# Low parts of the activations on GpSimd in four pieces, the second group's halves in the v part, 22 v passes beside u, and the samples' rstd a quarter step later

## The chip, the cores and the metric

One core of a Trainium2 chip. The metric is the device time of one execution in microseconds; it was 3186.38 for the kernel before (median of three). TensorE is PE, its weight loads PEld, VectorE DVE, ScalarE ACT, GpSimd POOL, SyncE SP.

## The reference

One decoder layer for 512 prompt tokens and 8 x 8 sample tokens (D = 2048), then a final RMSNorm. Cut to what matters here:

```
h  = rmsnorm(x) * (1 + scale1) + shift1;  x = x + gate1 * mix(h)      # RG-LRU and short conv, 1 projection in, 1 out
h2 = rmsnorm(x) * (1 + scale2) + shift2
# PEER: 8 heads, product keys 128 x 128 -> 16384 experts, top 16 per head
q    = (h2 @ w_q) per head, two halves of 128;  scores against 128 + 128 sub keys;  top 16 of the 256 sums
g    = softmax(top);  act = gelu(<h2, expert_u[eidx]>) * g
x    = x + gate2 * sum_k act_k * expert_v[eidx_k]
y    = rmsnorm(x)
```

expert_u and expert_v are 16384 x 2048 in fp32. All matrix products must come out in fp32 accuracy.

## The kernel before

The first 1160 us or so compute modulation, projections, scans and the output projection. The two parts after that hold the change.

**u part** (to about 2220 us). Of the 128 blocks of 128 experts, the L = 80 that the prompt's tokens pick most are computed densely. A block's rows of `ut` come in two half blocks n (0 to 159, NU2 = 160). `load` brings a half block into `raw` (SP queue, L892, 512 KB). `conv` splits it for PE, whose fp32r products are made of three passes: ACT writes the high part `xhi` (L908), POOL the low part `xlo = raw - xhi` (L909). `ahead(l, c)` issues loads up to l and conversions up to c, in order. `u_half` (L1405) multiplies 8 tiles three times each (hi*hi, hi*lo, lo*hi), 24 matmuls of 512 columns a half block. ACT applies gelu and writes the block's activations to DRAM (`actd`).

**Sparse rest.** Tokens whose picks lie in the other blocks, and the samples, are done by passes: POOL gathers 128 rows of 8 KB (`take`, L1235, an indirect DMA), DVE makes the dot product with h in a u pass (L1263), or adds the weighted row to `accB`, which is in PSUM, in a v pass (L1290). There are 219 uses of the u kind (NU; 214 of them are passes), then 214 v passes. `gather_to(k)` issues uses up to pass k, with gathers as far ahead as row buffers are free. From half block R2 = 129 on the passes are spread evenly: from G0 = 201 to NU + EARLY_V at the u part's end.

**v part** (from about 2220 us to 3151). M = 80 steps m of four quarter steps kq. A step takes four blocks and a quarter of the 2048 columns, as two half blocks n = 160 + 2m and the next; a quarter step is 12 matmuls (`v_column`, L1425), where the stationary side is `xhi` or `xlo` and the moving side the blocks' activations, `ahi` and `alo`. `v_sum` adds a finished bank to `acc` (DVE, L1447). Activations come in groups sg of four blocks (SG = 4, 20 groups). A group's work is a row of jobs, keyed by quarter step 4m + kq:

- `load_weights(sg, q)`, four loads of the gates into `gsb` (ACT queue, L1356); `load_acts(sg, q)`, two loads of the activations into `actr` (ACT queue, L1363). Both tiles have one buffer.
- `weigh(sg)`: `actr *= gsb` on DVE (L1368), three quarter steps before `halve`.
- `halve(sg, 0)`: `ahi` on ACT (L1375); `halve(sg, 1)`: `alo = actr - ahi` on DVE (L1379). `ahi` and `alo` have three buffers.

With h_ the quarter step of `halve(sg, 0)` (12, 28, 44, ... 284 for sg 2 to 19), `hi_at` is that of the group before. Groups 0 and 1 are done at the end of the u part, at half blocks 153, 154 and 158, 159. A step issues first its `ahead`, then at each quarter step the passes due there, the jobs, and the matmuls. Each engine's queue keeps the order of the code. The passes of the v part are spread by `room`, which takes WEIGH = 2.8 off a quarter step that is in `busy`.

**The tail.** `fplan` names the quarter steps at which the samples' end (`finish_b`) goes on by one piece. Its fifth piece is the matmul that spreads the samples' rstd (`token_norm`: `ph` from `rcfb`, L1474); `rcfb` is computed on DVE and ACT (L144 to L150) from the sums of the fourth (L1469). `last` is 73. In the last steps `load_x` brings the residual `xf` (into the buffers of `gsb` and `actr`) and `add_x` adds it on DVE (L1440).

Of the kernel before, what the change touches and what calls it, by code (L numbers as in the profile page):

```python
# [32 lines left out]
SG = 4  # L33
# [17 lines left out]
LAG = 4  # L51
FIRST_G = 6
PAIRS = 8
EARLY_V = 16
KEPT = 5
WEIGH = 2.8
PARTS = 2
# [20 lines left out]
def r32(ap):  # L78
    return ap.bitcast(F32)


def build(ctx, tc, A, O, dbg=None):
    nc = tc.nc
    V, S, PE, G = nc.vector, nc.scalar, nc.tensor, nc.gpsimd
# [792 lines left out]
    raws, parts, gsb, ahl, acts, pools = {}, {}, {}, {}, {}, {}  # L877
# [36 lines left out]
    def ahead(l, c):  # L914
        while at["l"] <= min(l, len(stream) - 1):
            load(at["l"])
            at["l"] += 1
        while at["c"] <= min(c, len(stream) - 1):
            conv(at["c"])
            at["c"] += 1  # L920
# [114 lines left out]
    def sample_twice():  # L1035

        for k0 in range(0, KD, 8):
            r, a = new_row(f"dup{k0}")
            row_log[a] = True
            d = r.bitcast(F32R).rearrange("p (q k t) -> p q k t", q=2, t=128)  # L1040
            dups.append(d)
            for q in range(2):
                S.activation(d[:, q].rearrange("p k (r t) -> p k r t", t=NG),
                             r32(hv[q][:, k0:k0 + 8, None, NA:T]).to_broadcast([128, 8, 2, NG]), AF.Copy)
# [306 lines left out]
    def load_weights(sg, q):  # L1351

        if q == 0:
            gsb[sg] = ep.tile([128, NCH, SG * TC], F32, name=f"gsb{sg}", tag="gsb", bufs=1)
        c = slice(q * NCH // GP, (q + 1) * NCH // GP)
        nc.scalar.dma_start(gsb[sg][:, c, :], gd[c, :, sg * SG:(sg + 1) * SG, :].rearrange("c p i t -> p c (i t)"))  # L1356
# [13 lines left out]
    def halve(sg, part):  # L1370

        if part == 0:
            pool = ep if sg % 3 < 2 else pools["vx"]
            hi, lo = (pool.tile([128, SG, NA], F32R, name=f"{x}{sg}", tag=f"{x}{sg % 3}", bufs=1) for x in ("ahi", "alo"))
            S.activation(hi, acts[sg], AF.Copy)  # L1375
            ahg[sg] = (hi, lo)
            return
        hi, lo = ahg[sg]
        V.tensor_sub(lo, acts.pop(sg), r32(hi))  # L1379
        for j in range(SG):  # L1380
            ahl[SG * sg + j] = (hi[:, j, :], lo[:, j, :])

    ahg = {}
# [259 lines left out]
    for n in range(NU2):  # L1643
        _, i, c = stream[n]
        if n == 0:
            sample_twice()
        if n == 1:
            sample_rows()
        ahead(n + 3, n + 2)
        spare += PIECE if R1 is None else PIECE_G  # L1650
        if R1 is not None:
            put(2)
            g_one(n)
            if not gk:
                g_start()
            elif gm[0] < min(upto(n), gm[1] + PAIRS - 1):
                g_pair(gm[0])
                gm[0] += 2
                spare -= 2.2
            while gm[2] < gm[3]:  # L1660
                g_scale(gm[2])
                gm[2] += 1
            gm[3], gm[4] = gm[4], gm[0]

        even, waits = R2 is not None, False
        while spare > 0 and R2 is None:
            cost = next(steps1 if R1 is None else steps2, "end")
            if cost == "end":
                if R1 is None:
                    R1 = n  # L1670
                else:
                    R2 = n
                break
            if cost is None:
                waits = True
                break
            spare -= cost
        if not even:
            if since is None and ready[0]:
                since = n  # L1680
            if since is not None and n == since + 1:
                fetch_to(RB - 1)
            if since is not None and n > since + 2:
                due_g += RATE[R1 is not None] + (0.7 if waits and spare > 4.5 else 0.0)
            g0 = gu[0]
            gather_to(due_g, ready[0])
            if gu[0] == ready[0] and sorted_[0]:
                fetch_to(gu[0] + 1, ready[0])
            due_g = min(due_g, gu[0] + 1.0)
            spare -= 2.4 * (gu[0] - g0)  # L1690
            if waits:
                spare = min(spare, 3.0)
            G0 = gu[0]
        else:
            gather_to(G0 + (NU + EARLY_V - G0) * (n - R2) // (NU2 - 1 - R2))
        if n == E0:
            assert not pair and not stg
            put(len(puts))
            p2.close()
            epx = ctx.enter_context(ExitStack())  # L1700
            ep = epx.enter_context(tc.tile_pool(name="ep", bufs=1))
        u_half(n, i, c)
        for sg, o in ((0, 1), (1, 7)):
            d = n - E0 - o
            if 0 <= d < 2:
                load_weights(sg, 2 * d)
                load_weights(sg, 2 * d + 1)
            if 2 <= d < 4:
                load_acts(sg, d - 2)
            if d == 5 - sg:  # L1710
                weigh(sg)
            if d == 6 - sg:
                halve(sg, 0)
            if d == 7 - sg:
                halve(sg, 1)
    hp_.close()
    vp = ctx.enter_context(tc.tile_pool(name="vp", bufs=1, side="right"))
    acc = vp.tile([128, KD, NA], F32, name="acc")
    pools["vx"] = ctx.enter_context(tc.tile_pool(name="vx", bufs=1, side="right"))
    NV0 = NU + EARLY_V  # L1720
    gather_to(NV0)
# [3 lines left out]
    last = M - VQ - ENDS  # L1725
    KQ = KD // VQ
    jobs, busy = {}, {}
    hi_at = -4
    for sg in range(2, L // SG):
        use = uses_of[sg * SG]  # L1730
        free = KQ * (uses_of[(sg - 3) * SG][-1] + 1) if sg >= 3 else 0
        h_ = min(KQ * use[0] - 7, max(free, hi_at + 16))
        assert h_ >= free and h_ >= hi_at + 13, (sg, h_, free, hi_at)
        for q in range(GP):
            jobs.setdefault(max(hi_at - 1 + q, 0), []).append(lambda sg=sg, q=q: load_weights(sg, q))
        for q in range(AP_):
            jobs.setdefault(max(hi_at + 5 + q, 0), []).append(lambda sg=sg, q=q: load_acts(sg, q))
        jobs.setdefault(h_ - 3, []).append(lambda sg=sg: weigh(sg))
        jobs.setdefault(h_, []).append(lambda sg=sg: halve(sg, 0))
        jobs.setdefault(h_ + 2, []).append(lambda sg=sg: halve(sg, 1))  # L1740
        busy[h_ - 3] = busy[h_ + 2] = WEIGH
        hi_at = h_
    room = {}
    for m in range(last):
# [1 line left out]
            room[m, kq] = PIECE / 2 - 0.75 * steps[m][4] - busy.get(KQ * m + kq, 0.0)  # L1746
    tot, run_ = sum(room.values()), 0.0
    fb = finish_b()
    fplan = {(last, 3), (last + 1, 2), (last + 1, 3), (last + 2, 1), (last + 2, 2), (last + 2, 3)}
    fin["tok"] = []  # L1750
    tplan = {(last + 1, 1), (last + 1, 2), (last + 1, 3), (last + 2, 0)}
    NT = len(uses)
# [2 lines left out]
    for m in range(M):  # L1755
        gi, q, bl, first, final = steps[m]
# [56 lines left out]
    with tc.If(any_ > 0), tc.tile_pool(name="fb", bufs=1) as fp:  # L1813
        io1 = fp.tile([128, 128], F32, name="f_io1")
        V.tensor_scalar(io1, iota, 1.0, None, op0=ALU.add)
        for i, (p0, n, c) in enumerate(GT):
# [18 lines left out]
            d = fp.tile([128, NPK], F32, name=f"f_d{i}", tag="d", bufs=1)  # L1835
            a = fp.tile([128, D], F32, name=f"f_a{i}", tag="a", bufs=1)
# [105 lines left out]
```

## Time and profile before

| | |
|---|---|
| runs | 3186.25, 3186.38, 3189.34 us |
| profiled execution | 3178.14 us |
| its span | 3176.2 us |
| mean granted clock of PE | 0.985 |
| u passes' dots, v passes' adds, DVE | 483.2 us (x214), 475.2 us (x202) |
| xlo, POOL, whole program | 773.8 us (x320) |
| alo and weigh, DVE | 20 each, medians 2.29 and 2.29 us |
| ahi, ACT | 20, median 1.90 us |

The profile is that of one execution, whose time lies 8.2 us below the median of the runs; its rows add up to its own time. An engine's row gives busy time, share of the span, and instructions. A group's row gives count, busy time, the mean in ns, and the idle time of the engine ahead of it with what ended it. A row of waits gives what an engine stood for: total us, times, longest. A window's row gives start and end, length, busy time of PE, PEld, DVE, ACT and POOL with their counts, the granted PE clock, the DMA share, and GB/s.

### The profile page before, as it was taken

Reading aid. Unit: us, or ns where it says so; the run is one execution under the profiler, and the core shown is the slowest. Engines: PE = TensorE matmul, PEld = TensorE weight load, DVE = VectorE, ACT = ScalarE, POOL = GpSimd, SP = SyncE. Lnnn points to the kernel's source line nnn. Section 1 sums busy time; section 2 is a strip of 40 time slices with the busy share of each in tenths; the row PEclk is TensorE's granted clock in tenths of the full one; section 3 lists DMA queues with packets and bytes.
Section 4 is the critical chain, followed back from the end, with each engine's and each line's share of the span. In section 5 each row is a group of like instructions: output and inputs, shape, how many; then the busy total and the mean of one; then the engine's idle time right before and its main releaser. Section 6 shows DMA issues by size and latency. Waiting matters only on the chain.

```text
span 3176.2 us, 46544 instructions
## 1 busy us (share of the span) xinstructions
PE 3060.1 (96%) x17239; PEld 2604.4 (82%) x17239; DVE 2123.5 (67%) x3240; ACT 1047.0 (33%) x1640; POOL 1681.4 (53%) x983
## 2 busy tenths in 40 slices
PE   5999999999989999999999999999999999999997
PEld 2688888899979998887888888887788888787776
DVE  3455621143254797986998999945677888888765
ACT  3234311123232223222555555652322222222222
POOL 2333333344333335667565666645766767777752
PEclk9999999999999999999999999999999999999998
DMA  9743566633332126989889999979999999899984
GB/s 386 281 138 136 180 206 212 214 127 131 126 114 102 67 82 216 310 307 384 339 333 387 393 380 393 384 278 373 380 382 356 380 376 376 302 388 378 374 294 154
DMA packets 294473, 882.81 MB, mean 278 GB/s; under 512 B 34998, under 2 KB 76854, under 8 KB 242774
## 3 DMA queue, kind: packets, MB, share of 16 engines
q1 hardware_dynamic: 160608, 380.39, 33.5%
q0 software_dynamic: 63744, 413.40, 32.7%
q10 hardware_dynamic: 69888, 86.00, 7.6%
q8 instruction: 136, 2.23, 0.3%
q14 instruction: 97, 0.79, 0.1%
HBM read 861.02 MB, written 66.81 MB: 292 GB/s over the span
## 4 chain that ended last, share of the span: by engine, by line
PE 68%; DMA 14%; POOL 6%; issue 5%; DVE 5%; ACT 1%; SPq 1%; ACTq 0%; POOLq 0%; DVEq 0%
PE pu L1405 17%; PE pv L1425 17%; PE pp_o L140 6%; DMA raw<-v 4%; DMA gsb<-gd 4%; PE pp_c L140 3%; PE pp_s L140 3%; POOL xlo L909 3%; PE qa L140 3%; PE pp_b L140 3%; PE qb L140 3%; PE pp_x L140 2%; PE pp_y L140 2%; PE ada L190 2%; DMA actr<-actd 2%
## 5 line engine op out<-in xcount | busy, mean ns | idle before, releaser
L909 POOL TENSOR_TENSOR xlo<-raw,xhi 128x1024 fp32r<-128x1024 f32 x320 | 773.8, 2427 | 424.2 <-ACT xhi L908 414.5
L908 ACT ACTIVATE xhi<-raw 128x1024 fp32r<-128x1024 f32 x320 | 338.1, 1061 | 862.5 <-PE pv L1425 311.4
L1263 DVE SCALAR_TENSOR_TENSOR u<-u,hT 128x2048 f32<-128x2048 f32 x214 | 483.2, 2282 | 104.3 <-DMA u<-u,rows 103.9
L1290 DVE SCALAR_TENSOR_TENSOR accB<-v,dots,accB 128x2048 f32<-128x2048 f32 x202 | 475.2, 2353 | 102.2 <-DMA v<-v,rows 99.0
L1425 PE MATMUL pv<-ahi,xhi 128*128 128x512 f32 x1280 | 509.6, 398 | 8.2 <-DVE acc L1447 5.4
L1405 PE MATMUL pu<-hhi,xhi 128*128 128x512 f32 x1280 | 515.0, 402 | 0.0
L1425 PE MATMUL pv<-ahi,xlo 128*128 128x512 f32 x1280 | 507.3, 396 | 6.3 <-POOL xlo L909 6.2
L1405 PE MATMUL pu<-hhi,xlo 128*128 128x512 f32 x1280 | 503.3, 393 | 1.6 <-POOL xlo L909 1.5
L1425 PE MATMUL pv<-alo,xhi 128*128 128x512 f32 x1280 | 504.2, 394 | 0.0
L1405 PE MATMUL pu<-hlo,xhi 128*128 128x512 f32 x1280 | 503.6, 393 | 0.0
L1235 POOL DMA_INDIRECT u<-u,rows x214 | 214.7, 1003 | 206.5 <-DVE u L1263 154.2
L1425 PEld LDWEIGHTS pv<-ahi,xlo 128*128 128x128 f32 x1280 | 242.2, 189 | 64.9 <-POOL xlo L909 8.7
L1425 PEld LDWEIGHTS pv<-ahi,xhi 128*128 128x128 f32 x1280 | 242.2, 189 | 64.5 <-DVE acc L1447 7.7
L1405 PEld LDWEIGHTS pu<-hhi,xlo 128*128 128x128 f32 x1280 | 241.1, 188 | 57.0 <-POOL xlo L909 2.8
L1425 PEld LDWEIGHTS pv<-alo,xhi 128*128 128x128 f32 x1280 | 242.6, 190 | 54.7
L1405 PEld LDWEIGHTS pu<-hhi,xhi 128*128 128x128 f32 x1280 | 241.7, 189 | 49.6 <-issue 0.9
L1405 PEld LDWEIGHTS pu<-hlo,xhi 128*128 128x128 f32 x1280 | 241.9, 189 | 48.5
L1235 POOL DMA_INDIRECT v<-v,rows x214 | 246.3, 1151 | 51.8 <-issue 33.9
L1599 ACT ACTIVATE op<-op,it 128x128 f32<-128x128 f32 x512 | 155.6, 389 | 40.3 <-DVE op L1591 40.2
L1605 PEld LDWEIGHTS gbank<-wr,op 128*128 128x128 f32 x1024 | 133.1, 191 | 21.4 <-ACT stg L1612 11.9
L1447 DVE TENSOR_TENSOR acc<-acc,pv 128x512 f32<-128x512 f32 x144 | 96.9, 682 | 76.7 <-PE pv L1425 76.7
L129 POOL TENSOR_TENSOR wlo_o<-raw_o,whi_o 128x1024 fp32r<-128x1024 f32 x32 | 77.5, 2423 | 119.9 <-ACT whi_o L127 115.9
(498 smaller groups left out, 5453.5 us busy)
## 6 DMA issues: line engine op xcount, KB each, us to landing
wa<-w_ada SPq DMA_DIRECT2D x96, 1024.0 KB, 7.5
raw<-ut SPq DMA_DIRECT2D x160, 512.0 KB, 7.9
raw<-v SPq DMA_DIRECT2D x320, 256.0 KB, 9.0
actd<-act ACTq DMA_DIRECT2D x80, 256.0 KB, 7.5
gd<-stg ACTq DMA_DIRECT2D x64, 320.0 KB, 12.3
gsb<-gd ACTq DMA_DIRECT2D x80, 256.0 KB, 14.4
actr<-actd ACTq DMA_DIRECT2D x40, 512.0 KB, 9.7
raw_o<-w_out SPq DMA_DIRECT2D x32, 512.0 KB, 3.4
```

Of the source, the lines that this page charges most:

```text
L129: lo_engine(share).tensor_sub(lo, raw, r32(hi))
L140: PE.matmul(o, st, mv[pick](k), start=first, stop=last)
L908: S.activation(hi, raw, AF.Copy)
L909: G.tensor_sub(lo, raw, r32(hi))
L1235: G.indirect_dma_start(out=out, out_offset=None, in_=src, in_offset=bass.IndirectOffsetOnAxis(ap=idx, axis=0), bounds_check=NE * 128 - 1, ...
L1263: V.scalar_tensor_tensor(r, r, 1.0, st["h"], op0=ALU.mult, op1=ALU.mult, accum_out=dots[i][:, j:j + 1])
L1290: V.scalar_tensor_tensor(st["a"], r, dots[i][:, j:j + 1], st["a"], op0=ALU.mult, op1=ALU.add)
L1405: PE.matmul(pu, st[:, kk, :], movA[mv](k), start=k == 0 and a == 0, stop=k == KD - 1 and a == 2)
L1425: PE.matmul(pv, st, mv, start=first and j == 0 and a == 0, stop=last and not end and j == SG - 1 and a == 2)
L1447: V.tensor_add(ak, ak, pv)
L1599: S.activation(ops[:, j0 + j, :], ops[:, j0 + j, :], AF.Copy, scale=it[2][:, b * 4 + j:b * 4 + j + 1])
L1605: PE.matmul(pg[:, j * L:(j + 1) * L], ops[:, j0 + j, :], wr[:, j0 + j, :], start=True, stop=True)
```

## The change

1. `EARLY_V` is 22 instead of 16: six more v passes end beside the u part (from n = 129 on 40 passes instead of 34), and 192 gathers of v remain after it instead of 198.
2. `halve`'s low part is made by POOL in pieces of one block (128 x 512), two pieces as part 1 and two as part 2 (L1380).
3. In the u part only group 0 is halved, at half blocks 153, 154 and 155. Group 1 is halved at quarter steps 1, 2 and 3 of the v part.
4. `hi_at` starts at -1 instead of -4, so `halve` comes a quarter step later for every group from 2 on (13, 29, 45, ... 285), at h_, h_ + 1 and h_ + 2. The gates' loads stand at hi_at - 1 + q, which are now the four quarter steps of one step (before, the first fell into the step ahead). `busy` holds weigh alone.
5. `fplan` has the samples' rstd at (last + 2, 3) instead of (last + 2, 2), and the piece after it at (last + 3, 1).

```diff
-EARLY_V = 16
+EARLY_V = 22
...
@@ halve
         hi, lo = ahg[sg]
-        V.tensor_sub(lo, acts.pop(sg), r32(hi))
-        for j in range(SG):
+        for j in range(SG // 2 * (part - 1), SG // 2 * part):
+            G.tensor_sub(lo[:, j, :], acts[sg][:, j, :], r32(hi[:, j, :]))
             ahl[SG * sg + j] = (hi[:, j, :], lo[:, j, :])
@@ u part, for sg, o in ((0, 1), (1, 7)): d = n - E0 - o
-            if d == 6 - sg:
-                halve(sg, 0)
-            if d == 7 - sg:
-                halve(sg, 1)
+            if 6 <= d < 9 and not sg:
+                halve(sg, d - 6)
@@ jobs of the v part
-    hi_at = -4
+    hi_at = -1
+    for a in range(3):
+        jobs.setdefault(1 + a, []).append(lambda a=a: halve(1, a))
...
-            jobs.setdefault(max(hi_at - 1 + q, 0), []).append(lambda sg=sg, q=q: load_weights(sg, q))
+            jobs.setdefault(max(hi_at - 1 + q, q), []).append(lambda sg=sg, q=q: load_weights(sg, q))
...
-        jobs.setdefault(h_, []).append(lambda sg=sg: halve(sg, 0))
-        jobs.setdefault(h_ + 2, []).append(lambda sg=sg: halve(sg, 1))
-        busy[h_ - 3] = busy[h_ + 2] = WEIGH
+        for a in range(3):
+            jobs.setdefault(h_ + a, []).append(lambda sg=sg, a=a: halve(sg, a))
+        busy[h_ - 3] = WEIGH
...
-    fplan = {(last, 3), (last + 1, 2), (last + 1, 3), (last + 2, 1), (last + 2, 2), (last + 2, 3)}
+    fplan = {(last, 3), (last + 1, 2), (last + 1, 3), (last + 2, 1), (last + 2, 3), (last + 3, 1)}
```

In the rows below the number behind a name is that of the half block, the group or the pass (`xlo157` is that of half block 157, `alo0` that of group 0, `v0_13` a gathered row of v); the number behind the underscore tells buffers apart. `x2` is two such instructions in a row.

POOL at the end of the u part, before:

```order
L909 TENSOR_TENSOR xlo157_20197<-raw157_20149,xhi157_20196 128x1024
L1235 DMA v0_13_20200<-v,rows0_8654 128x2048
L909 TENSOR_TENSOR xlo158_20240<-raw158_20191,xhi158_20239 128x1024
L1235 DMA v0_14_20243<-v,rows0_8654 128x2048
L909 TENSOR_TENSOR xlo159_20284<-raw159_20234,xhi159_20283 128x1024
```

and now:

```order
L909 TENSOR_TENSOR xlo156_20180<-raw156_20122,xhi156_20179 128x1024
L1235 DMA v0_17_20183<-v,rows0_8654 128x2048
L1380 TENSOR_TENSOR alo0_20169<-actr0_19994,ahi0_20168 128x512 x2
L909 TENSOR_TENSOR xlo157_20223<-raw157_20174,xhi157_20222 128x1024
L1235 DMA v0_18_20226<-v,rows0_8654 128x2048
L1380 TENSOR_TENSOR alo0_20169<-actr0_19994,ahi0_20168 128x512 x2
L909 TENSOR_TENSOR xlo158_20268<-raw158_20217,xhi158_20267 128x1024
L1235 DMA v0_19_20271<-v,rows0_8654 128x2048
L1235 DMA v0_20_20276<-v,rows0_8654 128x2048
L909 TENSOR_TENSOR xlo159_20317<-raw159_20262,xhi159_20316 128x1024
```

Two pieces of group 0 have come between `xlo156` and `xlo157`, two between `xlo157` and `xlo158`, and the gathers are those of four to six passes later.

DVE in the v part about group 13 (about 2745 to 2770 us), before:

```order
L1368 TENSOR_TENSOR actr13_24683<-actr13_24683,gsb13_24524 128x2048
L1290 SCALAR_TENSOR_TENSOR accB1_23993<-v1_27_24717,dots1_14473,accB1_23993 128x2048
L1290 SCALAR_TENSOR_TENSOR accB1_23993<-v1_28_24774,dots1_14473,accB1_23993 128x2048
L1290 SCALAR_TENSOR_TENSOR accB1_23993<-v1_29_24792,dots1_14473,accB1_23993 128x2048
L1447 TENSOR_TENSOR acc_20421<-acc_20421,pv6_4_24854 128x512
L1290 SCALAR_TENSOR_TENSOR accB1_23993<-v1_30_24849,dots1_14473,accB1_23993 128x2048
L1447 TENSOR_TENSOR acc_20421<-acc_20421,pv6_5_24868 128x512
L1379 TENSOR_TENSOR alo13_24951<-actr13_24683,ahi13_24950 128x2048
L1447 TENSOR_TENSOR acc_20421<-acc_20421,pv6_6_24886 128x512
L1447 TENSOR_TENSOR acc_20421<-acc_20421,pv6_7_24906 128x512
```

and the group's pieces now, on POOL:

```order
L909 TENSOR_TENSOR xlo256_24972<-raw256_24705,xhi256_24971 128x1024
L909 TENSOR_TENSOR xlo257_24976<-raw257_24792,xhi257_24975 128x1024
L1235 DMA v3_3_25012<-v,rows3_8660 128x2048
L1380 TENSOR_TENSOR alo13_25018<-actr13_24750,ahi13_25017 128x512 x2
L1235 DMA v3_4_25050<-v,rows3_8660 128x2048
L1305 DMA accd_8628<-v1_32_24859,tok_8651 512x2048
L1380 TENSOR_TENSOR alo13_25018<-actr13_24750,ahi13_25017 128x512 x2
L909 TENSOR_TENSOR xlo258_25076<-raw258_24801,xhi258_25075 128x1024
L909 TENSOR_TENSOR xlo259_25080<-raw259_24885,xhi259_25079 128x1024
```

`alo13` has left DVE, where it stood between two sums of finished banks, for POOL, where it follows the step's two xlo and precedes those of the next.

PE in step 75 (`pv9_13` and `pv9_14` are its quarter steps 1 and 2), before:

```order
L1425 MATMUL pv9_13_27531<-ahi18_26879,xhi311_27494 128x512
L1425 MATMUL pv9_13_27531<-alo18_26880,xhi311_27494 128x512
L1425 MATMUL pv9_13_27531<-ahi18_26879,xlo311_27495 128x512
L1474 MATMUL ph_27544<-ident_76,rcfb_27642 128x64
L1425 MATMUL pv9_14_27567<-ahi18_26879,xhi310_27490 128x512
```

and now:

```order
L1425 MATMUL pv9_14_27627<-ahi18_26951,xhi311_27554 128x512
L1425 MATMUL pv9_14_27627<-alo18_26952,xhi311_27554 128x512
L1425 MATMUL pv9_14_27627<-ahi18_26951,xlo311_27555 128x512
L1474 MATMUL ph_27604<-ident_76,rcfb_27702 128x64
L1425 MATMUL pv9_15_27646<-ahi18_26951,xhi310_27550 128x512
```

The matmul that spreads the rstd stands behind the 12 of quarter step 2 instead of the 12 of quarter step 1.

## The prediction

> **What bounds the kernel now.** I read the engine totals first, then windows of the last stage, then what TensorE waited for, then the chain at those places. The engine totals of the page:
>
> ```profile
> PE 3060.1 (96%) x17239; PEld 2604.4 (82%) x17239; DVE 2123.5 (67%) x3240; ACT 1047.0 (33%) x1640; POOL 1681.4 (53%) x983
> ```
>
> PE is busy for 96% of the span, so an edit off PE can win only what PE waits, and what its clock loses behind a wait. All edits lie between 2050 us and the end. The windows there (window, length, busy us of PE, PEld, DVE, ACT, POOL with counts, granted clock, DMA share, GB/s):
>
> ```profile
> 2120.00:2140.00 20.00, 20.00 (x101) 16.84 (x100) 5.72 (x6) 6.62 (x9) 11.22 (x8) 1.00 0.62 205
> 2200.00:2220.00 20.00, 19.91 (x87) 15.98 (x86) 10.31 (x5) 6.89 (x7) 13.85 (x8) 1.00 1.00 373
> 2220.00:2240.00 20.00, 16.81 (x60) 12.85 (x59) 11.92 (x6) 5.23 (x7) 13.94 (x8) 0.83 0.93 349
> 2300.00:2340.00 40.00, 40.00 (x175) 32.58 (x174) 29.53 (x20) 10.30 (x9) 26.76 (x18) 1.00 1.02 386
> 2620.00:2660.00 40.00, 40.00 (x175) 32.57 (x175) 36.65 (x20) 9.68 (x10) 34.64 (x21) 1.00 0.95 361
> 2740.00:2780.00 40.00, 35.47 (x141) 28.04 (x140) 31.73 (x16) 9.46 (x9) 27.86 (x17) 0.91 0.91 330
> 2860.00:2900.00 40.00, 37.99 (x162) 30.01 (x162) 31.87 (x18) 8.02 (x7) 26.54 (x18) 1.00 0.99 373
> 3020.00:3060.00 40.00, 36.24 (x155) 28.60 (x154) 34.11 (x20) 10.30 (x9) 26.91 (x14) 1.00 0.81 309
> 3080.00:3100.00 20.00, 17.04 (x73) 13.66 (x73) 9.71 (x17) 3.19 (x5) 6.84 (x3) 0.91 0.66 214
> ```
>
> An undisturbed window holds 175 matmuls in 40 us, 0.2286 us each; a step of 48 is 11.0 us, a group's four steps (192) are 43.9 us. Missing matmuls are lost time: 34 in 2740:2780 (7.8 us), 20 in 3020:3060 (4.6), 13 in 2860:2900 (3.0), 27.5 in 2220:2240 (6.3). What PE waited for between 2160 and 3160 us (us in total, times, longest):
>
> ```profile
> PE pv L1425 <- POOL xlo L909: 6.2, 4, 1.7
> PE pv L1425 <- DVE acc L1447: 5.4, 3, 3.5
> PE ph L1474 <- DVE rcfb L150: 3.0, 1, 3.0
> PE pv L1425 <- ACT xhi L908: 2.6, 3, 1.5
> ```
>
> That is all there is to win: 17.2 us of waits, and the clock behind the longest: 0.83 of 20 us (3.4 us lost), 0.91 of 40 (3.6), 0.91 of 20 (1.8). So 26 us at most, less at most whatever the change adds.
>
> **The change, part by part.** The sum stands against the profiled execution, 3178.1 us, which is 8.2 under the median 3186.4; I add the 8.2 back at the end.
>
> *The samples' rstd behind 12 more matmuls.* The chain at that place (start, us):
>
> ```profile
> 3070.12 14.02 DMA xf<-x1d
> 3084.16 0.75 DVE acc L1440
> ...
> 3086.19 0.43 PE ph L1474 x2
> 3086.62 10.09 PE pv L1425 x36
> ...
> 3097.60 2.79 PE pv L1425 x12
> ```
>
> PE stood 3.0 us at L1474 since rcfb on DVE followed acc L1440, which followed a transfer. Then 36 matmuls took 10.09 instead of 3 x 2.79 = 8.4: 1.7 us of clock. With 12 more matmuls ahead the wait shrinks by 2.79 to 0.2; 2860:2900, with waits of 1.7 and less, kept a clock of 1.00. Nothing else in the tail waits for ph within a quarter step. -4.5 (ends: 0 if the transfer lands 3 us later, -4.7).
>
> *alo off VectorE.* Around the longest wait, DVE's rows, then POOL's, then one link of the chain:
>
> ```profile
> 2757.99 2.36 DVE L1290 SCALAR_TENSOR_TENSOR accB<-v,dots,accB 128x2048 f32<-128x2048 f32 x1 [3.11 <-DMA v<-v,rows]
> 2760.25 0.68 DVE L1447 TENSOR_TENSOR acc<-acc,pv 128x512 f32<-128x512 f32 x1
> 2760.85 6.53 DVE L1379 TENSOR_TENSOR alo<-actr,ahi 128x2048 fp32r<-128x2048 f32 x1
> 2767.30 1.27 DVE L1447 TENSOR_TENSOR acc<-acc,pv 128x512 f32<-128x512 f32 x2
> ```
>
> ```profile
> 2760.49 4.74 POOL L909 TENSOR_TENSOR xlo<-raw,xhi 128x1024 fp32r<-128x1024 f32 x2
> 2765.38 2.87 POOL L1235 DMA_INDIRECT v<-v,rows  x1 [0.16 <-issue]
> ```
>
> ```profile
> 2719.80 25.07 DMA actr<-actd
> ```
>
> alo stood ahead of two acc that PE needed for its banks, and took 6.53 us because POOL's two xlo ran until 2765.2; the gather behind them took 2.87 while alo ran. With alo elsewhere the acc comes at 2760.9 instead of 2767.3, and the 3.5 us wait goes with its clock (3.5 of the 3.6). The other two waits on acc, 1.9 us, I leave: no row puts them behind alo. What is late next is weigh, for which actr's 25 us landing is as late as before; it holds VectorE, but acc is then one accB behind, not one alo. -7 (ends: -2, when that landing alone decides; -9.0, all of 5.4 and 3.6).
>
> *alo on GpSimd.* Prices (groups, and the tile):
>
> ```profile
> L909 POOL TENSOR_TENSOR xlo<-raw,xhi 128x1024 fp32r<-128x1024 f32 x320 | 773.8, 2427 | 424.2 <-ACT xhi L908 414.5
> L1235 POOL DMA_INDIRECT v<-v,rows x214 | 246.3, 1151 | 51.8 <-issue 33.9
> L318 POOL TENSOR_TENSOR w1hs<-w1r,w1xc 128x512 fp32r<-128x512 f32 x4 | 5.1, 1277 | 29.7 <-ACT w1xc L317 29.7
> ```
>
> ```profile
> L1379 DVE TENSOR_TENSOR alo<-actr,ahi x20: 2283/2290/6528, 2194.6 to 3037.2; 128x2048 fp32r<-128x2048 f32 x20
> ```
>
> L318 is the same subtraction in a piece's size: 4 x 1.28 = 5.1 us a group, for 2.29 on VectorE. GpSimd's densest window is 2620:2660, 34.64 of 40, so 38.0 of a group's 43.9; with the pieces 43.1. It gets back what alo took from it, 1.9 where a gather took 2.87 for 0.99: 41.2 of 43.9. Elsewhere (26.76 of 40) there is more room. While it waits for ahi, its xlo would wait too, but the next xhi stands behind that ahi on ScalarE anyway. So nearly hidden. The last pieces are issued five quarter steps (13.7 us) ahead of their first matmul or more, and three (8.2 us) ahead of the next load into actr, which has one buffer. With the gsb loads issued in one step in place of two: +1.5 (ends: 0, and +25 below).
>
> *Six passes fewer in the v part.* 214 passes less 16 are 198 there; less 22, 192. Six are 6 x 128 rows x 8 KB = 6.3 MB, 16 us of the transfers at 386 GB/s, in some 850 us of a stage in which they run at 0.9 to 1.0: 2% less. PE's waits on xlo and xhi are 8.8 us, of which 3.2 lie at the transition (below); the other 5.6 come from raw that landed late, and can shrink. -3, about half, since 2% shortens a queue that is just full by more than 2% (ends 0, -5.6). The passes move into the last 170 us of the u part, where 2120:2140 has a DMA share of 0.62 and DVE 5.72 of 20: nothing, up to the last 20 us, which are at 1.00.
>
> *The transition.* ScalarE's rows, GpSimd's, and one link of the chain:
>
> ```profile
> 2203.08 0.34 ACTq L1363 DMA_DIRECT2D actr<-actd  x1
> 2203.46 1.06 ACT L908 ACTIVATE xhi<-raw 128x1024 fp32r<-128x1024 f32 x1 [2.16 <-POOL xlo L909]
> ...
> 2221.46 1.06 ACT L908 ACTIVATE xhi<-raw 128x1024 fp32r<-128x1024 f32 x1 [3.89 <-DMA raw<-v]
> ```
>
> ```profile
> 2200.90 2.39 POOL L909 TENSOR_TENSOR xlo<-raw,xhi 128x1024 fp32r<-128x1024 f32 x1 [5.55 <-ACT xhi L908]
> ...
> 2204.61 2.40 POOL L909 TENSOR_TENSOR xlo<-raw,xhi 128x1024 fp32r<-128x1024 f32 x1 [0.17 <-ACT xhi L908]
> ```
>
> ```profile
> 2207.86 13.58 DMA raw<-v
> ```
>
> The first half block of v that PE multiplies second is read after the xlo of 2204.61 ends at 2207.0, lands at 2221.4, and PE waits 3.2 us, first for xhi, then for xlo:
>
> ```profile
> PE pv L1425 <- POOL xlo L909: 1.7, 1, 1.7
> PE pv L1425 <- ACT xhi L908: 1.5, 1, 1.5
> ```
>
> In the new order two pieces stand between the xlo of 2200.90 and that of 2204.61 (2.6 us), and the actr load at 2203.08 now waits for them, with the next xhi (1.06) behind it on ScalarE. So that xlo ends some 4 us later (2.6 + 1.06, and the issues between), the read starts 4 later, and PE waits 7 instead of 3. That the second group's ahi leaves the u part helps nothing here: the xhi of 2221.46 waited for its transfer. +4 (ends: 0 if the landing falls into a quieter queue, +7 if the 13.58 grows by another 3).
>
> Sum: -4.5 - 7 + 1.5 - 3 + 4 = -9.0, so 3169.1 profiled, 3177.4 on the median: **3177 us**.
>
> **A rule against a row.** The clock cost above is taken from the granted clock. The Trainium skill, page "TensorE: Matmul & The Clock Gate", Part 1, says that the clock falls to half for a window of 3.4 us, free-running, so a wait would cost some 1.7 us behind it. 3080:3100 agrees with it (1.8); 2220:2240 and 2740:2780 show 3.4 and 3.6, two windows. By that rule alo's term would be -5.2, and the time 3179.
>
> **The rivals.**
>
> *GpSimd becomes the pace (slower).* For it: 43.1 of 43.9 in the densest window, and POOL's waits:
>
> ```profile
> POOL xlo L909 <- ACT xhi L908: 184.2, 61, 9.2
> ```
>
> 184.2 us from 2220 to 3060 are 9.6 a group. If a third of that (3.2) can't be squeezed out, because xhi waits for PE to free its buffers, and alo gives nothing back, a group needs 43.1 + 3.2 = 46.3: 2.4 too many in each of the 10.5 groups from 2600 to 3060 us, 25 us. With the other terms (-10.5): +14.5, 3201. It decides once a group overruns by 1.0 us. Against it: the 1.9 given back, and windows like 2300:2340. The Trainium skill, "SBUF — State Buffer", "Who interferes with whom", says that a VectorE instruction with at most one SBUF input, outside the 2-port modes, doesn't contend with GpSimd; by it accB, whose sum lies in PSUM, leaves the pieces alone. The mean xlo, 2427 ns, doesn't contradict it, and no row here shows the pieces beside accB.
>
> *The transfers decide (no change).* The v part runs at 361 to 386 GB/s, and late transfers start each of its stalls. Then 2% less buys nothing, alo's place is taken by the next thing on VectorE (-2), the transition costs its 4, the tail gives 4.5, GpSimd 1.5: -1.0, 3185. For it: DMA shares of 0.93 to 1.02. Against: at 2760.85 VectorE was ready for the acc that PE needed, and did alo for 6.53 us first.
>
> *All waits in the v part go.* -4.7 - 9.0 - 5.6, and no cost at the transition: -19.3, 3167. For it: stalls are few and short, and a little slack may end them all. Against: the transition's order.
>
> **Chances.** Forecast 0.42 (own range 3171 to 3183), transfers decide 0.27, GpSimd's pace 0.18, all waits gone 0.13. A measurement here tells from no change what is beyond 0.2%, 6.4 us: below 3180.0 and above 3192.8. Three quarters of the forecast's case lie below 3180 (0.32), with 0.13 and 0.03 of the transfers' case: faster 0.48; slower 0.18; same 0.34. The range, 3165 to 3197, leaves out half of the slower case and a part of the fastest.
>
> **What would show it.** PE's wait for rcfb at L1474 under 0.5 us and the clock 1.00 in the window that holds it; PE's waits on acc at 2 us or less in total; pieces at L1380 of 1.3 us each, and xlo not over 2.5; POOL some 38 to 39 of 40 in its densest window; a wait of some 7 us at the v part's start, on xhi or xlo. I am wrong if PE waits for xlo group after group, in step with the pieces (GpSimd's pace), if acc is still late behind weigh, or if the first wait of the v part is no longer than 3 us.

## The result, and the profile after

The changed kernel took 3161.57 us (median of 6 runs), the kernel before beside it 3186.59: ratio 0.9923 (95% interval 0.9906 to 0.9939). A second set gave 3166.45 against 3183.56, ratio 0.9937 (0.9918 to 0.9957). So 17 to 25 us faster, two to nearly three times the 9 forecast. The first set lies 3.4 us under the stated range, the second inside it.

The traced executions show less. They took 3178.1 and 3173.4 us for the kernel before, 3168.7 and 3172.3 for the changed one: 5 us apart on the mean. Of the twelve runs behind this repeat of the kernel before, the traced one is the shortest (3173.4, the others to 3199.3); of the six of each set of the changed kernel, it is the longest. Some of that lies ahead of the change, in code that it leaves as it was: PE began the u part at 1196.4 us in the first trace of the changed kernel (1192.5 and 1189.8 in those of before), and in the second it took 838.7 us for the half blocks ahead of 129 (833.3 and 832.9 before; from PE's start times). So what a trace of these two kernels shows is the smaller part of the gain; the larger part I can place only by runs of edited kernels.

The page of the changed kernel, to be held against the same lines of before:

```profile
PE 3061.4 (97%) x17239; PEld 2602.8 (82%) x17239; DVE 2060.1 (65%) x3220; ACT 1045.5 (33%) x1640; POOL 1772.1 (56%) x1063
...
L909 POOL TENSOR_TENSOR xlo<-raw,xhi 128x1024 fp32r<-128x1024 f32 x320 | 774.7, 2434 | 323.5 <-ACT xhi L908 309.7
```

VectorE lost 63 us, GpSimd gained 91, and GpSimd's idle time ahead of xlo fell from 424 to 324 us: the pieces went into waits. PE's waits from 2160 to 3160 us (total, times, longest):

```profile
PE pv L1425 <- POOL xlo L909: 5.9, 7, 1.2
PE pu L1405 <- POOL xlo L909: 3.5, 2, 1.8
...
PE ph L1474 <- DVE rcfb L150: 0.3, 1, 0.3
```

The waits on acc (5.4) are gone in this trace, and that for rcfb (3.0) nearly. Windows of the changed kernel, then, over the 800 us from 2240 to 3040, of the kernel before:

```profile
2620.00:2660.00 40.00, 40.00 (x175) 32.58 (x174) 30.18 (x21) 8.10 (x8) 35.65 (x24) 1.00 1.02 396
2740.00:2780.00 40.00, 40.00 (x175) 32.54 (x175) 28.39 (x19) 9.58 (x10) 36.07 (x23) 1.00 0.96 347
3080.00:3100.00 20.00, 19.67 (x103) 16.40 (x102) 13.39 (x21) 5.06 (x8) 5.20 (x2) 1.00 0.69 229
2240.00:3040.00 800.00, 793.84 (x3432) 643.32 (x3432) 572.83 (x348) 193.37 (x183) 654.07 (x415) 1.00 0.98 368
```

```profile
2240.00:3040.00 800.00, 788.67 (x3396) 638.75 (x3395) 634.54 (x366) 190.88 (x180) 569.80 (x340) 1.00 0.98 371
```

2740:2780 is full (175 matmuls, 141 before), 3080:3100 has a clock of 1.00. Over the 800 us PE did 36 matmuls more (8.2 us), while the transfers ran at the same share, 0.98: they were full before and are full now. The second traces of the two kernels show no such difference (3409 and 3410 matmuls), so a pair of traces is thin evidence here.

### The profile page after: what moved, and what is told of

It reads as the page before. It is cut to its first block, busy times and chain, and to the rows that moved or that the text cites. A ratio compares the mean times of both kernels' runs of the same rounds, so it can differ in the third digit from the quotient of the medians.

```text
span 3166.9 us, 46617 instructions
## 1 busy us (share of the span) xinstructions
PE 3061.4 (97%) x17239; PEld 2602.8 (82%) x17239; DVE 2060.1 (65%) x3220; ACT 1045.5 (33%) x1640; POOL 1772.1 (56%) x1063
## 3 DMA queue, kind: packets, MB, share of 16 engines
q0 software_dynamic: 63744, 413.40, 33.0%
## 5 line engine op out<-in xcount | busy, mean ns | idle before, releaser
L909 POOL TENSOR_TENSOR xlo<-raw,xhi 128x1024 fp32r<-128x1024 f32 x320 | 774.7, 2434 | 323.5 <-ACT xhi L908 309.7
L1290 DVE SCALAR_TENSOR_TENSOR accB<-v,dots,accB 128x2048 f32<-128x2048 f32 x202 | 475.2, 2353 | 123.4 <-DMA v<-v,rows 121.7
L1235 POOL DMA_INDIRECT v<-v,rows x214 | 235.0, 1098 | 49.3 <-issue 33.8
L1447 DVE TENSOR_TENSOR acc<-acc,pv 128x512 f32<-128x512 f32 x144 | 97.4, 683 | 144.1 <-PE pv L1425 144.1
```

The lines of the kernel that those rows point to most:

```text
L909: G.tensor_sub(lo, raw, r32(hi))
L1235: G.indirect_dma_start(out=out, out_offset=None, in_=src, in_offset=bass.IndirectOffsetOnAxis(ap=idx, axis=0), bounds_check=NE * 128 - 1, ...
L1290: V.scalar_tensor_tensor(st["a"], r, dots[i][:, j:j + 1], st["a"], op0=ALU.mult, op1=ALU.add)
L1447: V.tensor_add(ak, ak, pv)
```

## The experiments

Each line is the median of n runs; the difference is to the median of the kernel before on the same chip, the ratio has its 95% interval. The ratio is not that of the two medians, and can stand a few us beside the difference (e8: -24.4 us, and 0.9941, which is -18.8).

| run | edit | us (n) | difference | ratio |
|---|---|---|---|---|
| n1_before | none | 3184.1 (12) | -0.1 | 1.0001 (0.9984 to 1.0017) |
| e1_alo_pool | alo in pieces on GpSimd, alone | 3180.7 (12) | -3.6 | 0.9985 (0.9968 to 1.0003) |
| e2_early22 | 22 early passes, alone | 3178.1 (12) | -6.1 | 0.9980 (0.9965 to 0.9994) |
| e3_rstd_later | rstd later, alone | 3178.3 (12) | -6.0 | 0.9981 (0.9964 to 0.9998) |
| e7_later_halves | halves and gates' loads later, alone | 3188.0 (12) | +4.5 | 1.0008 (0.9989 to 1.0026) |
| e4_alo_back | changed, alo on VectorE | 3171.4 (12) | -12.1 | 0.9967 (0.9949 to 0.9985) |
| e5_early16 | changed, 16 early passes | 3190.0 (12) | +6.4 | 1.0016 (0.9999 to 1.0033) |
| e6_group1_back | changed, group 1 in the u part | 3160.6 (6) | -22.9 | 0.9929 (0.9904 to 0.9953) |
| e12_no_later | changed, without the later halves | 3159.4 (6) | -25.9 | 0.9911 (0.9882 to 0.9940) |
| e15_rstd_back | changed, rstd as before | 3165.0 (7) | -20.3 | 0.9934 (0.9910 to 0.9958) |
| e13_early19 | changed, 19 early passes | 3166.5 (9) | -18.9 | 0.9937 (0.9915 to 0.9959) |
| e8_early28 | changed, 28 early passes | 3162.2 (6) | -24.4 | 0.9941 (0.9919 to 0.9963) |
| e9_half_gathers | e5, 12 half gathers (5.4 MB less) | 3175.6 (12) | -11.0 | 0.9975 (0.9960 to 0.9991) |
| e14_before_half_gathers | before, 12 half gathers (5.4 MB less) | 3163.3 (8) | -22.0 | 0.9937 (0.9914 to 0.9960) |
| e10_gates_spaced | changed, gates' loads spaced | 3166.0 (6) | -20.6 | 0.9944 (0.9924 to 0.9965) |
| e11_early16_spaced | e5, gates' loads spaced | 3181.4 (12) | -5.2 | 0.9993 (0.9979 to 1.0006) |
| e16_no_later_28 | e12 with 28 early passes | 3168.9 (6) | -14.7 | 0.9946 (0.9927 to 0.9965) |
| n2_after | changed, again | 3166.5 (6) | -17.1 | 0.9937 (0.9918 to 0.9957) |

### One part alone

**The kernel before, again.** No edit.

> The kernel before once more, unchanged, for a second profile and the scatter of its runs. Theory A (its one profile is typical): PE's waits from 2160 to 3160 us are again some 17 us, with the 3.0 us at rcfb and one wait of over 3 us on acc, and the time is the same within 0.2%. Theory B (that profile was a lucky one: its time lay 8.2 us under the median): the v part of this profile has some 25 us of waits, most of them for late halves of v (xlo, xhi).

The time is the same. The runs of one kernel spread over 26 us (3173.4 to 3199.3), as much as the whole change is worth. PE's waits from 2160 to 3140 us:

```profile
PE pv L1425 <- ACT xhi L908: 6.4, 2, 4.4
PE pv L1425 <- DVE acc L1447: 5.1, 3, 2.6
PE pv L1425 <- POOL xlo L909: 2.9, 2, 1.7
PE ph L1474 <- DVE rcfb L150: 2.6, 1, 2.6
```

17.0 us again, in other places, with no wait on acc over 3 us: Theory A by the sum. But this execution too was 11 us shorter than the median, so neither trace is that of a usual run.

**alo alone.**

```diff
-        V.tensor_sub(lo, acts.pop(sg), r32(hi))
+        for j in range(SG // 2 * (part - 1), SG // 2 * part):
+            G.tensor_sub(lo[:, j, :], acts[sg][:, j, :], r32(hi[:, j, :]))
...
```

The two parts stand at h_ + 1 and h_ + 2, and `busy` holds weigh alone, as in the change.

> The kernel before with one edit: alo in four pieces on GpSimd (two a quarter step behind ahi, two a quarter step later; for groups 0 and 1 all four at the half block where alo stood). Theory A: the waits on acc and the clock behind the longest go, -9 us, 3177; nothing else changes. Theory B (VectorE's alo was also what made gathers and xlo late): -15 or more, 3171. Rival (GpSimd becomes the pace): waits on xlo grow with the pieces, 3190 or more.

-3.6, an interval that holds 0. In the trace the waits on acc are gone as expected, and those for late halves are as long as they were (9.2 us for xlo and xhi; 8.8 and 9.3 in the two traces of before):

```profile
PE pv L1425 <- POOL xlo L909: 7.1, 5, 1.7
PE ph L1474 <- DVE rcfb L150: 3.9, 1, 3.9
PE pv L1425 <- ACT xhi L908: 2.1, 2, 1.8
```

PE stood 13.3 us in all for 17, and the time fell by no more than that: Theory A's 9, with the clock, is not reached. alo was the last in line at the waits on acc; that it made PE late beyond them isn't shown.

**22 early passes alone.** `EARLY_V = 22`.

> The kernel before with one edit: 22 v passes beside the u part instead of 16. Theory A: 0 to -3 us, since only late halves of v gain by it. Theory B (the transfers of the v part are the larger part of its waits): -8 or more, 3178 or less. Rival (transition): the last 20 us of the u part are at a DMA share of 1.0, so the first wait of the v part grows by 2 to 4 us and the time is 3187 to 3190.

-6.1, between the two theories. Of the rival the longer first wait came, but not its time. In this trace the first step of the v part pays:

```profile
PE pv L1425 <- ACT acc L1445: 7.5, 1, 7.5
```

ScalarE's rows there, the gates' loads of group 2 (L1356), then activations' loads (L1363), with the copies of finished banks behind them (L1445):

```profile
2227.74 5.58 ACTq L1356 DMA_DIRECT2D gsb<-gd  x4
...
2235.01 0.34 ACTq L1363 DMA_DIRECT2D actr<-actd  x1
2235.40 0.60 ACT L1445 ACTIVATE acc<-pv 128x512 f32<-128x512 f32 x1 [1.44 <-DMA raw<-v]
2247.49 0.34 ACTq L1363 DMA_DIRECT2D actr<-actd  x1
2247.87 1.09 ACT L1445 ACTIVATE acc<-pv 128x512 f32<-128x512 f32 x2 [11.88 <-DMA gsb<-gd]
```

The second load could be issued only at 2247.5, when a gates' transfer had landed; the copy behind it on ScalarE stood for 11.9 us, and PE for 7.5.

**rstd later alone.** `fplan` as in the change.

> The kernel before with one edit: the samples' rstd a quarter step later (and the piece after it). Theory A: the wait at L1474 falls from 3.0 us to 0.2 to 0.5 and the clock behind it stays at 1.00: -4.5 us, 3182. Rival: the wait goes but the end is set by another chain (xf, acc), 0 us.

-6.0 (0.9964 to 0.9998), which holds the expected 4.5. PE's wait for rcfb was 0.4 us.

**Later halves alone.** `hi_at = -1`, group 1 at quarter steps 1 and 3, loads at `max(hi_at - 1 + q, q)`; alo whole on VectorE.

> The kernel before with one part of the change alone: groups 2 on halved a quarter step later, group 1 in the v part, the gates' loads spread over the four quarter steps of one step; alo stays whole on VectorE, 16 early passes, rstd as before. Theory A: what the three other parts leave of the 25, -9 us, 3176. Theory C: 0, 3184, since it only pays with the pieces on GpSimd. Rival: slower, 3187 or more, since four loads of gates stand in one step.

+4.5 (0.9989 to 1.0026): no gain; Theory C (0) and the rival (slower) can't be told apart. The four parts alone add up to -11.2, of 17 to 25, each with 5 to 6 us to either side.

### One part undone

**alo back on VectorE**, in the four pieces (`V.tensor_sub` for `G.tensor_sub`).

> The changed kernel with one edit undone: alo's four pieces on VectorE instead of GpSimd, at the same places. Theory A (the parts add up: alo alone gave 4, the v passes 6, the rstd 6 of the 25): 3161 + 4 = 3165. Theory C (the parts need each other: the pieces on GpSimd pay only once the halves come later): 3170 or more, waits on acc L1447 back at 3 us or more. Rival (GpSimd's pieces cost what they give): 3161 or less.

3171.4, -12.1: 5 to 13 us of the change are lost, more than alo was worth alone. That fits Theory C by the time, but not by its sign: waits on acc L1447 were 1.1 us in this trace, where PE waited for xhi (4.5), xlo (4.1) and ScalarE's copies at L1445 (3.9). The pieces, here on VectorE and in the changed kernel on GpSimd:

```profile
L1380 DVE TENSOR_TENSOR alo<-actr,ahi x80: 675/686/4068, 2194.4 to 3039.9; 128x512 fp32r<-128x512 f32 x80
```

```profile
L1380 POOL TENSOR_TENSOR alo<-actr,ahi x80: 1283/1302/1346, 2198.0 to 3038.8; 128x512 fp32r<-128x512 f32 x80
```

**16 early passes.** `EARLY_V = 16` in the changed kernel.

> The changed kernel with one edit undone: 16 v passes beside the u part instead of 22. Theory A: 3161 + 6 = 3167. Theory C: 3172 or more, since GpSimd's pieces need the room. Rival (the passes moved forward are worth nothing): 3161 within 3.

3190.0: by the differences 24 to 31 us lost, all of the change (that it is slower than before is not clear of the noise). One wait for xhi was 12.4 us. ScalarE's loads of the gates, then its rows up to that wait:

```profile
L1356 ACTq DMA_DIRECT2D gsb<-gd x80: 366/447/12372, 2150.7 to 3002.0; - x80
```

```profile
2798.93 11.54 ACTq L1356 DMA_DIRECT2D gsb<-gd  x2
2810.59 2.24 ACT L908 ACTIVATE xhi<-raw 128x1024 fp32r<-128x1024 f32 x2 [10.04 <-issue]
2832.44 5.67 ACTq L1363 DMA_DIRECT2D actr<-actd  x2
2838.23 3.90 ACT L908 ACTIVATE xhi<-raw 128x1024 fp32r<-128x1024 f32 x4 [25.39 <-DMA actr<-actd]
```

Two issues held the queue for 11.5 us, where one takes 0.37 at the least and 0.45 in the median; the next load waited until 2832, and four xhi with it. The changed kernel at the same place:

```profile
2801.11 9.95 ACTq L1356 DMA_DIRECT2D gsb<-gd  x2
2811.17 2.01 ACT L908 ACTIVATE xhi<-raw 128x1024 fp32r<-128x1024 f32 x2 [10.20 <-issue]
2815.94 3.86 ACTq L1363 DMA_DIRECT2D actr<-actd  x2
2819.92 2.01 ACT L908 ACTIVATE xhi<-raw 128x1024 fp32r<-128x1024 f32 x2 [6.74 <-DMA actr<-actd]
```

The same block is there, 18 us shorter, and hidden. The transfers were full in both, at a share of 1.03 (16 passes) and 1.05 from 2800 to 2820 us.

**Group 1 back in the u part** (ahi at half block 158, four pieces at 159, no jobs for it in the v part).

> The changed kernel with one edit undone: group 1 is halved in the u part again (ahi at half block 158, the four pieces at 159). Theory A or C: the first step of the v part gets longer, 3164 to 3168, and PE's wait for xhi or xlo at the start of the v part is 4 us or more. Rival (place of group 1 is worth nothing, as its ahi only stood where xhi waited for its transfer anyway): 3161 within 3.

3160.6: the rival. The place of group 1 is worth nothing that can be measured.

**No later halves.** The kernel before with e1's, e2's and e3's edits.

> The kernel before with three parts of the change (alo in pieces on GpSimd, 22 early passes, the rstd later), but the halves of groups 1 on and the gates' loads where they were. Theory A (the parts add): 3185 - 4 - 6 - 6 = 3169. Theory F (the later halves are worth nothing once 22 passes are ahead): 3158 to 3164. Theory G (they are worth 10 or more): 3172 or more.

3159.4: Theory F; and three parts that give 15.7 alone give 26 together, though with some 9 us to either side of each sum this alone doesn't show that they help each other. PE's waits in the v part are down to:

```profile
PE pv L1425 <- POOL xlo L909: 2.6, 3, 1.7
...
PE ph L1474 <- DVE rcfb L150: 1.2, 1, 1.2
PE pv L1425 <- ACT acc L1445: 0.9, 1, 0.9
```

It is the fastest version here, with a smaller edit than the change; against the changed kernel (0.9923, 0.9937) the intervals overlap.

**rstd back** in the changed kernel.

> The changed kernel with the samples' rstd a quarter step earlier again. By the wait at L1474 (3.0 us) and its clock (1.7): 3161 + 4.5 = 3166, the wait back at 2.5 to 4 us. Rival: with the passes ahead the chain to rcfb ends earlier, the wait is under 1 us and the time 3161 to 3163.

The wait came back, 3.8 us, as expected. The time, -20.3, can't be told from the changed kernel's -17.1 and -25.0.

### The bytes

**Half gathers with 16 passes.** In e5's kernel, 12 gathers of the v part are:

```diff
+            if gf[0] >= NU + 40 and gf[0] % 14 == 0 and 0 < j < c - 1:
...
+                take(held[j][0][:, :D // 2], A["v"].rearrange("r (a c) -> (r a) c", a=2), rows_i[i][:, j:j + 1])
```

and their adds read the half row twice.

> The changed kernel with 16 early passes (3190), and 12 of the v part's 198 gathers fetch 128 x 4 KB instead of 128 x 8 KB (their adds run over the half row twice, so GpSimd and VectorE have as much to do): 6.3 MB less, as many bytes as six passes, with no pass moved. It leaves out half of the data of these 12 passes. Theory D (bytes): 3161 to 3170. Rival (a pass's work on GpSimd and VectorE is what 22 took out of the v part): 3187 to 3192.

3175.6, 14.4 under e5 (17.4 when each is held against the kernel before in its own set): between the two. The expectation's 6.3 MB is the edit's count of full rows; the gathers' queue moved 5.4 MB less (413.40 MB in e5, 407.99 here). At e5's 360 GB/s that is 15.0 us, and about half of what 22 passes brought there.

**Half gathers in the kernel before.** The same edit on the kernel before.

> The kernel before with 12 of its v part's gathers at 128 x 4 KB instead of 128 x 8 KB: 6.3 MB less, no pass moved, no order changed. It leaves out half of the data of these 12 passes. Theory D (bytes are the pace of the v part in the old order too): -14 as in the changed kernel with 16, 3170; then moving six passes alone (-6) lost 8 at the transition. Rival (the old order has room, the bytes are only dear in the new one): -6 or less, 3179 or more.

3163.3: -22.0 (0.9914 to 0.9960, -13 to -27), more than Theory D's -14, which the interval holds. Here too the gathers' queue moved 5.4 MB less (packets, MB, share of the 16 DMA engines; before, then here):

```profile
q0 software_dynamic: 63744, 413.40, 32.7%
```

```profile
q0 software_dynamic: 63744, 407.99, 32.5%
```

At before's 371 GB/s that is 14.6 us. The engines had as much to do as before: a gather took GpSimd 1160 ns in the mean (1151 before), and each of the twelve adds over a half row took VectorE 2353 ns, as a whole one does. So fewer bytes alone, with no instruction moved, alo on VectorE and the rstd early, give as much as the whole change. PE's waits from 2160 to 3100 us (L1434 is here the line of `v_column`, L1483 that of the rstd):

```profile
PE pv L1434 <- POOL xlo L909: 3.4, 2, 1.7
PE ph L1483 <- DVE rcfb L150: 3.0, 1, 3.0
PE pv L1434 <- ACT xhi L908: 1.4, 1, 1.4
```

No wait on acc is left, with alo where it was: in this trace alo on VectorE made PE wait for nothing. (That alo was late in the kernel before because the transfers were is my reading; no run isolates it.) This traced execution is the shortest of the eight, 3.5 us under their median. The window from 2240 to 3040 us:

```profile
2240.00:3040.00 800.00, 798.28 (x3461) 649.44 (x3461) 636.32 (x374) 190.89 (x177) 574.99 (x344) 1.00 0.97 367
```

Still a share of 0.97, but PE is busy for all but 1.7 us.

**19 early passes.**

> The changed kernel with 19 v passes beside the u part (16 gave 3190, 22 gave 3161, 28 gave 3162). Theory D as a slope (each pass some 4.7 us until PE is the pace): 3175. As a threshold (stalls of 5 us and more begin at some amount of bytes): 3190 or 3161, within 5 of one of the two.

-18.9: with 16, 19, 22 and 28 passes +6.4, -18.9, -25.0 (-17.1 the second time) and -24.4. That is much nearer to a threshold than to a slope: nearly all of the gain comes with the first three passes, and then it is flat. Three passes are 3.1 MB at most, 8.7 us at 360 GB/s, and brought 25 us; so the gain is not in proportion to the bytes.

**28 early passes.**

> The changed kernel with 28 v passes beside the u part instead of 22. Theory D (the v part's transfers set its pace up to some amount of bytes: 16 passes gave 3190, 22 gave 3161): PE's waits in the v part are some 6 us with 22, so no more than 5 are left, and the last 20 us of the u part are full: 3156 to 3165. Rival A (each six passes are worth 6): 3155. Rival: the u part's end pays, 3168 or more.

3162.2, as Theory D had it; PE's wait for xlo in the u part was 4.9 us (3.5 and 2.0 in the two traces with 22).

**28 passes without the later halves.**

> The kernel before with alo in pieces on GpSimd, the rstd later and 28 early passes (later halves left out). Theory D (bytes, with a floor where PE is the pace): 3159 gave 22, the floor is near: 3153 to 3159. Rival (the u part's end pays for six more): 3162 or more.

3168.9, the rival: in its trace PE waits 8.0 us for ScalarE's copies (L1445) at the v part's start, as in e2.

### The gates' loads

**Gates' loads spaced**, in the changed kernel and with 16 passes:

```diff
-            jobs.setdefault(max(hi_at - 1 + q, q), []).append(lambda sg=sg, q=q: load_weights(sg, q))
+            jobs.setdefault(max(hi_at - 1 + 2 * q, q), []).append(lambda sg=sg, q=q: load_weights(sg, q))
-            jobs.setdefault(max(hi_at + 5 + q, 0), []).append(lambda sg=sg, q=q: load_acts(sg, q))
+            jobs.setdefault(max(hi_at + 6 + q, 0), []).append(lambda sg=sg, q=q: load_acts(sg, q))
```

> The changed kernel with the four loads of a group's gates two quarter steps apart instead of one (two in each of two steps; the loads of the activations a quarter step later). Theory E (ScalarE's queue is held by its own loads when four are under way, as in the 9.95 us of an issue near 2801 us, and xhi stands behind): the long issues on ScalarE go, 3156 to 3160. Rival: with 22 early passes that is hidden already, 3161 within 2.

> The changed kernel with 16 early passes (3190) and the gates' loads spaced as in the run before. Theory E (the burst on ScalarE's queue makes 16 passes so dear): 3165 to 3175, no wait for xhi of 5 us or more. Theory D (the bytes alone): 3185 to 3190, the waits lie elsewhere.

With 22 passes nothing (-20.6), and the longest issue of a gates' load was still 9.2 us. With 16 passes -8.6 against e5 (-11.6 by the differences), between Theory E and Theory D: the longest issue was 3.2 us (12.4 in e5) and no wait for xhi is left, but 13.8 us on acc L1447, one wait of them 8.0, and 6.5 for ScalarE's copies stand in its place. The burst on ScalarE's queue sets where a full transfer queue stops PE, and only part of how long.

**The changed kernel again.** No edit.

> The changed kernel once more, unchanged: 3158 to 3166, and PE's waits from 2160 to 3140 us are 6 to 10 us, none over 2.5.

3166.45, a touch over, and the expectation on the waits was missed. PE's waits in this trace: 5.7 us for xlo (longest 3.8) and 3.0 once on acc, so two waits over 2.5, and 11.3 us in all with those in the u part: a run with full queues can still stop PE.

## Why the prediction was wrong, point by point

**The step that failed is "six passes fewer in the v part", -3, with ends 0 and -5.6.** I saw the transfers full (shares of 0.93 to 1.02) and priced 6.3 MB at 16 us of them, and then counted only the 5.6 us that one trace showed PE waiting for late halves. Moving the six passes alone gave -6.1 (e2), a little past that end, and undoing it in the changed kernel cost 24 to 31 (e5). What the term left out are the bytes: with nothing else changed, 5.4 MB less gave -22 in the old order (e14) and -14 to -17 in the new one with 16 passes (e9), where they take 14.6 to 15.0 us at the rates shown. So the 16 us that I had as a side remark (14 to 15, with 5.4 MB for 6.3) were nearer to the price than the waits of one trace. They are not a law: three passes brought 25 us and the next nine nothing that can be measured (e13, e8), and 9 to 12 us of what 16 passes cost hang on the burst of gates' loads (e11).

Moving the six passes alone gives less than taking bytes away, since the start of the v part pays. By PE's start times e2's trace took 783.6 us for the steps 5 to 74 (795.7 and 792.9 in the two traces of before, 780.6 in e14), but 1098.9 from the first matmul of the u part to step 5 (1088.9 and 1090.2 before).

**The ceiling of 26 us was that of a short execution.** "All there is to win" came from a trace 8.2 us under the median. Both traces of before hold 17 us of waits; the usual run must lose some 10 us more, which no trace here shows in its place. The clocks on record point at PE: of 115 further runs of the kernel before, the 19 under 3178 us were granted 0.986 in the mean, the 12 over 3193 us 0.982, and 0.004 of 3180 us are 13 us, if PE was at work then (an estimate). I used the 8.2 only as an offset. The rival that came nearest, "all waits in the v part go", 3167, was priced with the same ceiling; that the second set came out at 3166.45 is luck, since over 9 us of waits were left in the v part of its trace.

**The samples' rstd: right.** Forecast -4.5; alone -6.0 (-0.6 to -11.5 by its interval), the wait 0.3 to 0.4 where 0.2 was forecast, the clock 1.00 in 3080:3100. In the changed kernel the wait comes back without this part (3.8 us, e15), but its time can't be told there.

**alo off VectorE: sign right, cause wrong.** Forecast -7 for this term and +1.5 for GpSimd. Alone both together gave -3.6, the waits on acc gone and those for late halves as before; taking it out of the changed kernel (e4) cost 5 to 13. The waits on acc do not hang on alo's place: e14 is without them with alo on VectorE, and n2 (3.0 us) and e11 (13.8) have them with alo on GpSimd. Where alo on GpSimd then saves time beside fewer bytes (e4) isn't shown; the stretched pieces on VectorE (up to 4.07 us) are near at hand, but I have no run that isolates them.

**alo on GpSimd: price right, nearly hidden.** Pieces of 1302 ns (1277 forecast), xlo 2434 ns, 35.65 and 36.07 of 40 in the densest windows (38 to 39 forecast). Four of PE's seven waits for xlo in the v part, 3.1 us together where the term had +1.5, came at two xlo that stood straight behind two pieces, near 2250 us and here:

```profile
2995.89 2.55 POOL L1380 TENSOR_TENSOR alo<-actr,ahi 128x512 fp32r<-128x512 f32 x2
2998.38 4.72 POOL L909 TENSOR_TENSOR xlo<-raw,xhi 128x1024 fp32r<-128x1024 f32 x2
```

That is twice in 20 groups; GpSimd's pace, 0.18, did not come.

**The transition: +4 forecast, 0 in the sum.** There are stalls, but earlier, two waits for xlo of 3.5 us together in the u part's last half blocks. ScalarE's rows there, then GpSimd's:

```profile
2194.40 10.70 ACTq L1356 DMA_DIRECT2D gsb<-gd  x1
2205.23 1.06 ACT L908 ACTIVATE xhi<-raw 128x1024 fp32r<-128x1024 f32 x1 [10.91 <-issue]
...
2212.86 1.06 ACT L908 ACTIVATE xhi<-raw 128x1024 fp32r<-128x1024 f32 x1 [6.08 <-POOL alo L1380]
```

```profile
2209.89 2.55 POOL L1380 TENSOR_TENSOR alo<-actr,ahi 128x512 fp32r<-128x512 f32 x2
2214.05 2.36 POOL L909 TENSOR_TENSOR xlo<-raw,xhi 128x1024 fp32r<-128x1024 f32 x1 [1.61 <-issue]
```

The first wait (1.7 us) came behind one issue of a gates' load, which held ScalarE for 10.7 us, and not behind the pieces. The second (1.8) is as I had it: the actr load waits for the pieces, xhi stands behind it, and xlo behind xhi. The start of the v part, where I put 7 us, lost little; PE's first waits there were 0.3 to 0.7 us, one of the signs of being wrong that I had named. From the first matmul of the u part to that of step 5 the traces took 1088.9 and 1090.2 us before, 1090.3 and 1094.3 after (from PE's start times): +2.8 on the mean, but that lies in the second trace's slow half blocks ahead of 129. From half block 129 on it is 255.6 and 257.3 before, 256.6 and 255.6 after: what the u part's end lost, 4 to 5 us, the first steps of the v part got back.

**The rule and the row.** Two waits of the changed kernel's second trace bear on the clock's price: one of 3.0 us in the first window below, one of 3.8 in the second.

```profile
2600.00:2620.00 20.00, 17.04 (x75) 13.60 (x74) 12.16 (x10) 3.64 (x4) 17.02 (x12) 1.00 0.80 277
2975.00:2995.00 20.00, 16.21 (x60) 12.46 (x59) 13.17 (x8) 4.98 (x4) 15.28 (x9) 0.83 1.02 391
```

After 3.0 the clock stayed at 1.00, after 3.8 it lost 3.4 us. So a wait of 3 us cost a clock of 1.8 in the kernel before and nothing here. The Trainium skill ("TensorE: Matmul & The Clock Gate", Part 1) has a window that runs freely, and with it such a wait may fall either way; the 3.4 us lost after the longer one are two such windows at half clock, 1.7 us each, as in the rows of before.

What stays open: what PE waits for in the longer runs of the kernel before, which no trace here caught; how the 17 to 25 us divide among the parts; and whether alo on GpSimd is worth more beside 22 passes (5 to 13 us) than alone (3.6), with some 5 us of noise to either side.

## What to carry to other kernels

When a stage's transfers run at a share of 0.97 and PE waits only here and there, price an edit first by the bytes that it takes out of the stage, in us at the rate shown, and not by the waits that one trace shows. Take it as a first price only: here 15 us of bytes gave 14 to 22, and the first three passes gave more than theirs. Stop when PE is the pace, since beyond that point fewer bytes give nothing (28 passes against 22). Watch an engine that issues transfers from its own queue: ScalarE here passed the full transfers on to everything behind the issue (xhi stood 10 us behind two of them). And look at how one traced time stands to the median before it is used as a ceiling.

## What the runs showed of the hardware

- The rate of this mix of transfers stayed where it was: share 0.96 to 0.98 and 360 to 372 GB/s from 2240 to 3040 us in all twenty traces, whether PE was busy for 773 us of the 800 (e5, the row below) or for 799 (e12: 0.97, 368).

```profile
2240.00:3040.00 800.00, 773.40 (x3308) 625.84 (x3309) 564.06 (x340) 181.04 (x171) 628.57 (x399) 0.98 0.96 360
```

- Two issues of loads on ScalarE's queue, 0.37 us each at the least, took 10 to 11.5 us with others under way, and held the engine's arithmetic behind them; the longest single one took 12.4 us (e5).
- A 128 x 512 subtraction with both inputs in SBUF took 675 to 4068 ns on VectorE beside GpSimd's xlo, and 1283 to 1346 ns on GpSimd: slower, and steady. The Trainium skill, "SBUF — State Buffer", "Who interferes with whom", says that a VectorE instruction with two SBUF inputs contends with a GpSimd instruction that reads SBUF. The 4068 agrees, and so does the changed kernel, where it was VectorE's small product of dots and gwt that grew: 2.33 us for 128 x 45 beside two pieces, 0.19 for 128 x 34 beside none. Beside accB, whose sum lies in PSUM, nothing grew: in the changed kernel's first trace 37 accB (2.34 to 2.36 us) overlapped 51 pieces (1.29 to 1.32), which the prediction had no row for.
